# A hybrid decoder block on one core: the order of copies and exponentials in cross attention, xo weights split on Pool, an earlier row load, and down's sums on VectorE

## Chip, core and metric

The kernel runs on one core of a Trainium2 chip. The metric is the device time of one launch in microseconds (us), the median of the runs. TensorE is called PE here, VectorE DVE, ScalarE ACT, GpSimd Pool, and SyncE, which issues nearly all DMAs, SP.

## What is computed

One layer (DEPTH = 1) with sequence 1024 and width 1024, all float32, in three sub-layers, each with an RMSNorm before and after and a residual. Only the second and the third are touched.

```python
def memory_cross_attention(h, mem_n, w_xq, w_xkv, w_xo):   # 4 heads of 256, 256 memory tokens
    q = (h @ w_xq).reshape(bsz, seq, 4, 256)
    k, v = _split(mem_n @ w_xkv, (1024, 1024))
    ...
    s = jnp.einsum('bshd,bmhd->bhsm', q, k) * (256 ** -0.5)
    p = jax.nn.softmax(s, axis=-1)
    o = jnp.einsum('bhsm,bmhd->bshd', p, v).reshape(bsz, seq, 1024)
    return o @ w_xo

def swiglu(h, w_gu, w_down):                               # hidden 2816
    gate, up = _split(h @ w_gu, (2816, 2816))
    return (jax.nn.silu(gate) * up) @ w_down

    ...
    x = x + rms_norm(merged @ w_mix_out[l], g_post_mix[l])
    h = rms_norm(x, g_pre_xa[l])
    mem_n = rms_norm(mem, g_mem[l])
    x = x + rms_norm(memory_cross_attention(h, mem_n, w_xq[l], w_xkv[l], w_xo[l]), g_post_xa[l])
    h = rms_norm(x, g_pre_ffn[l])
    x = x + rms_norm(swiglu(h, w_gu[l], w_down[l]), g_post_ffn[l])
```

## The kernel before

**Arithmetic.** A float32 operand is held as two parts: `hi`, the operand copied into a tile of type float32r, and `lo`, the operand less `hi`. A product is three matmuls: hi by hi, hi by lo, lo by hi (`mm3`, `acc3`). So nearly every operand costs one copy (`hi_sb`: ACT for "a", Pool for "p", DVE for "v") and one subtraction (`lo_of`, L122, on DVE unless another engine is named). Where two operands are split together, one instruction covers both.

The large products (q, gate and up, and down) are taken as 2 x 2 blocks with seven products in place of eight (Strassen's scheme in Winograd's form). Their operands are sums and differences of blocks, formed before the split.

**Cross attention.** A chunk is 128 rows of the sequence; there are eight. `soft(c)` computes a chunk's scores, two heads at a time into one PSUM tile (`sc`, four buffers). DVE takes the maximum (TENSOR_REDUCE) and scales it (TENSOR_SCALAR on two elements), ACT takes two exponentials with their sums. `normed` divides a chunk's probabilities by their sums (a reciprocal and one multiplication of 1024 elements). `turn_(half, h)` transposes the probabilities of a head for four chunks through PSUM (`tr`, two buffers), and ACT and DVE split them. `mix(half, h)` multiplies them with the values into PSUM banks (`mm`, two buffers), and ACT (copy) and DVE (subtraction) split the result `h`. The order is soft 0 to 5, turn (0,0), soft 6, turn (0,1), soft 7, and then mix of one head and turn of the head after the next by turns. In this stretch, and in the lead-ins below, `in_turn(True)` makes DVE, ACT and PE keep the order in which the program lists their work (line 49 is the helper that issues it). Elsewhere a scheduler orders each engine's queue when the kernel is built.

The output projection `out_proj` needs the eight row blocks of `w_xo`, split by `xo_weight(k)` with two buffers for the raw rows (`wraw`). Blocks 0 to 3 are split on Pool ahead of the scores. Blocks 4 to 7 go into the place of the queries (`qP`), and come last in the program, on ACT and DVE.

**Output projection and lead-in.** `out_proj` runs twice, for two halves of four chunks. A chunk loads its row of x, multiplies, takes the mean square (ACT), the reciprocal root (Pool, `rstd`), scales (DVE, L1457), adds the row (L1459), stores, normalises for the next sub-layer, and transposes. The last chunk's generator `run` is left in the list `late`, and the next sub-layer's `lead_in` runs its steps between the first products of that sub-layer. Its first step is the load of its row of x. `behind(marks)` makes an instruction issue after the marked ones. The weights' quarters come by `load` and `more`, one DMA of 512 KB each, on SP.

**Down.** The hidden width is 22 blocks of 128. Blocks 0 and 1, and 20 and 21, are multiplied plainly (`plain`, on operands from `whole_rows`). The other 18 go in three calls of `group`, each with three pairs of blocks. A group runs the products 1, 5, 6, 3, 7, 2, 4 in this order. A product has 36 matmuls on 12 combinations of pair and chunk, after which `add_to` (L2165) adds the PSUM banks to the result `a` on DVE. `operands` forms the sums (`sf`, five buffers) on Pool (L2071 to L2087; in the first group half of those of products 5 and 6 on DVE) and splits them into `op` (six buffers, so two products). The raw blocks lie in `gr` and `dr`, four buffers each. `last_tiles` loads and splits blocks 20 and 21 (`ol`) in the third group, before its product 3. `done` and `finish` are the last normalisation and the store.

Of the kernel before, what the change touches and what calls it, by code (L numbers as in the profile page):

```python
# [54 lines left out]
def hybrid_block(ctx, tc, a, out, dbg=None):  # L55
# [1552 lines left out]
    def lead_in(hb, xf, pa, pb, q, nq, sfp, swp, y, n00, ny, last, nlast, open_ps, open_tx, loaded):  # L1608
# [46 lines left out]
        with behind([loaded]):  # L1655
            next(run)
# [76 lines left out]
    with ExitStack() as q2:  # L1733
# [12 lines left out]
        with ExitStack() as xs:  # L1746
            sfp = pool(xs, "qsf", 4, side="right")
            swp = pool(xs, "qsw", 6, side="right")
            psl = ExitStack()

            def open_tx():
                q1.close()
                return pool(xs, "qtx", 2, side="right")

            def open_ps():
                psx.close()
                return pool(psl, "psl", 1, PSUM)

            def load(q, kh, c0):
                loads.append(quarter_load(q, w_xq, kh, c0 * P))  # L1760
                return quarter(q)

            def more(kh, c0):
                with behind(loads[-1:]):
                    return load(mk(t4, [P, S], F32, "x4"), kh, c0)

            loads = []
            spare = [qP[i].rearrange("p b s -> p (b s)")[:, HALF:HALF + S] for i in (3, 2, 0, 1)]
            n11, n12, q12, q21 = [load(r, kh, c0) for r, (kh, c0) in zip(spare, ((0, 4), (1, 4), (1, 0), (0, 2)))]
            lead_in(hx, xf, xa, xb, (lambda: more(0, 0), q12, q21, lambda: more(1, 2)), (n11, n12, lambda: more(0, 6), lambda: more(1, 6)), sfp, swp,  # L1770
                    rows_of(0), [qT[4 + p][:, 0:HALF] for p in range(2)], lambda: rows_of(4), fourth(2), fourth(6), open_ps, open_tx, loads[-1])
            psl.close()
# [17 lines left out]
        def xo_weight(k, hi_eng, lo_eng):  # L1790
            raw = mk(wbig, [P, D], F32, "wraw", 2)
            nc.sync.dma_start(raw, a["w_xo"][0][k * P:(k + 1) * P, :])
            hi_sb(wxo[k][:, 0], raw, hi_eng)
            lo_of(wxo[k][:, 1], raw, wxo[k][:, 0], lo_eng)

        for k in range(KT // 2):
            xo_weight(k, "p", G)
# [4 lines left out]
        sums, todo = {}, []  # L1802
# [7 lines left out]
        def soft(c):  # L1810
            mx = mk(stats, [P, 4], F32, "mx", bufs=4)
            sums[c] = mk(stats, [P, 4], F32, "sm", bufs=4)
            for h2 in range(2):
                ps = mk(psm, [P, 2, ML], F32, "sc", 4)
                for j in range(2):
                    h = 2 * h2 + j
                    for k in range(2):
                        T.matmul(ps[:, j, :], qT[2 * h + k][:, c * P:(c + 1) * P], kT[:, 2 * h + k, :], start=k == 0, stop=k == 1)
                m = mx[:, 2 * h2:2 * h2 + 2]
                V.tensor_reduce(m, ps, mybir.AxisListType.X, ALU.max)  # L1820
                V.tensor_scalar(m, m, -sc, None, ALU.mult)
                for j in range(2):
                    h = 2 * h2 + j
                    A.activation(prob[c][:, h, :], ps[:, j, :], AF.Exp, scale=sc, bias=mx[:, h:h + 1], accum_out=sums[c][:, h:h + 1])
                if h2 == 0:
                    normed()
            todo.append(c)
# [3 lines left out]
        def turn_(half, h):  # L1831
            for mt in range(2):
                pt = mk(psm, [P, HALF], F32, "tr")
                for ci in range(4):
                    T.transpose(pt[:, ci * P:(ci + 1) * P], prob[half * 4 + ci][:, h, mt * P:(mt + 1) * P], ident)
                t = mk(ptp, [P, 2, HALF], F32R, "pT") if h % 2 else mk(ld, [P, 2, HALF], F32R, "sw")
                A.activation(t[:, 0], pt, AF.Copy)
                V.tensor_tensor(t[:, 1], pt, t[:, 0].bitcast(F32), ALU.subtract)
                pT[half, h, mt] = t[:, 0], t[:, 1]
            normed()  # L1840

        def mix(half, h):
            for d in range(2):
                kk = 2 * h + d
                po = bank()
                for mt in range(2):
                    mm3(po, vh[mt][:, kk * P:(kk + 1) * P], vl[mt][:, kk * P:(kk + 1) * P], *pT[half, h, mt], mt == 0, mt == 1)
                hi, lo = ox[half][kk // 4]
                A.activation(hi[:, kk % 4, :], po, AF.Copy)
                V.tensor_tensor(lo[:, kk % 4, :], po, hi[:, kk % 4, :].bitcast(F32), ALU.subtract)  # L1850
                normed()
# [8 lines left out]
        soft(7)  # L1860
        steps = [(half, h) for half in range(2) for h in range(4)]
# [4 lines left out]
        wxo += [mk(qp, [P, 2, D], F32R, f"bw{k}") for k in range(KT // 2, KT)]  # L1866
        for k in range(KT // 2, KT):
            xo_weight(k, "a", V)
# [29 lines left out]
    with ExitStack() as q4:  # L1898
# [45 lines left out]
        n11 = load(fg[:, 0], 0, 2 * P)  # L1944
        q12 = more(1, 0)
# [7 lines left out]
        def later_results():  # L1953
# [4 lines left out]
                y, n00, later_results, both_gated(y, 0, "xk0"), both_gated(ny, 2, "xk1"), open_ps, open_tx, loads[-1])  # L1958
# [17 lines left out]
    with ExitStack() as q5:  # L1976
# [62 lines left out]
        def group(fs, first, end=None):  # L2039
            raws = []  # L2040
            for f in fs:
                raws.append((mk(rw, [P, 2, S], F32, "gr"), mk(rw, [P, 2, D], F32, "dr")))
                for r, src in zip(raws[-1], (gu_d, w_dn)):
                    if first:
                        nc.sync.dma_start(r[:, 0, 0:HALF], src[f * P:(f + 1) * P, 0:HALF])
                    else:
                        nc.sync.dma_start(r, rows(src, f, 2))
            if first:
                for f, rs in zip(fs, raws):
                    for r, src in zip(rs, (gu_d, w_dn)):  # L2050
                        nc.sync.dma_start(r[:, 0, HALF:], src[f * P:(f + 1) * P, HALF:])
                        nc.sync.dma_start(r[:, 1, :], src[(f + 1) * P:(f + 2) * P, :])
            lo_, hi_ = slice(0, HALF), slice(HALF, S)
            quarter = {}
            for i, (g, d) in enumerate(raws):
                quarter[i] = dict(a11=g[:, 0, lo_], a21=g[:, 0, hi_], a12=g[:, 1, lo_], a22=g[:, 1, hi_],
                                  b11=d[:, 0, lo_], b12=d[:, 0, hi_], b21=d[:, 1, lo_], b22=d[:, 1, hi_])

            E_ = V if first else G
# [4 lines left out]
            def operands(i, nm):  # L2064
                q = quarter[i]
                o = mk(op, [P, 2, 2, HALF], F32R, "op")
                if nm == "1":
                    src = q["a11"], q["b11"]
                elif nm == "5":
                    t = q["5"] = tmp()  # L2070
                    G.tensor_tensor(t[:, 0], q["a21"], q["a22"], ALU.add)  # L2071
                    E_.tensor_tensor(t[:, 1], q["b12"], q["b11"], ALU.subtract)
                    src = t
                elif nm == "6":
                    t = q["6"] = tmp()
                    G.tensor_tensor(t[:, 0], q["5"][:, 0], q["a11"], ALU.subtract)
                    E_.tensor_tensor(t[:, 1], q["b22"], q["5"][:, 1], ALU.subtract)
                    src = t
                elif nm == "3":
                    t = q["3"] = tmp()  # L2080
                    G.tensor_tensor(t[:, 0], q["a12"], q["6"][:, 0], ALU.subtract)
                    G.tensor_tensor(t[:, 1], q["b21"], q["6"][:, 1], ALU.subtract)
                    src = t[:, 0], q["b22"]
                elif nm == "7":
                    t = tmp()
                    G.tensor_tensor(t[:, 0], q["a11"], q["a21"], ALU.subtract)
                    G.tensor_tensor(t[:, 1], q["b22"], q["b12"], ALU.subtract)  # L2087
                    src = t
                elif nm == "2":
                    src = q["a12"], q["b21"]  # L2090
                elif nm == "4":
                    src = q["a22"], q["3"][:, 1]
# [33 lines left out]
            product(pa_, "6", False, False, [(0, 1)])  # L2126
            if end is None:
# [7 lines left out]
            tiles = end()  # L2135
# [41 lines left out]
        def rstd_c(c):  # L2177
            if c % 2 == 0:
                xts3[c // 2] = mk(rw, [P, 2, D], F32, ["gr", "dr"][c // 2 % 2])
# [12 lines left out]

        def last_tiles():
            f = NF - 2
            raws = mk(rw, [P, 2, S], F32, "gr"), mk(rw, [P, 2, D], F32, "dr")
            for r, src in zip(raws, (gu_d, w_dn)):
                nc.sync.dma_start(r, rows(src, f, 2))
            return [whole_rows([r[:, j] for r in raws]) for j in range(2)]

        gpost = load_gain(gpool, "g_post_ffn")  # L2200
        for g0 in range(NFIRST, NF - 2, 6):
            group([g0, g0 + 2, g0 + 4], g0 == NFIRST, last_tiles if g0 + 6 == NF - 2 else None)
# [31 lines left out]
```

## Time and profile before

| | |
|---|---|
| median of 3 runs | 2535.71 us (2533.68 to 2536.29) |
| the profiled execution: time, span | 2529.79 us, 2528.0 us |
| busy: PE, DVE, ACT, Pool | 97%, 72%, 46%, 32% of the span |
| cross attention from the first scores | about 1714 to 1781 us of the span |
| its output projection | about 1781 to 1872 us |
| lead-in of FFN, gate and up | 1872 to 2297 us |
| down | 2297.5 to 2528 us |

A matmul of 512 columns starts 0.227 us after the one before it when PE never waits. Rows of instructions give the start in us from the span's beginning, the duration, the engine, the line, the operation, the tiles as out<-in, shapes, and in square brackets the engine's idle time before the instruction with what ended it. "x2" means that two instructions are merged into one row.

### The profile page before, as it was taken

What the parts mean: (1) busy time and instruction counts of PE and PEld (TensorE: products, weight loads), DVE (VectorE), ACT (ScalarE), POOL (GpSimd) and SP (SyncE); (2) the same over time, 40 slices, a digit from 0 to 9 for tenths busy, and PEclk for the clock granted to TensorE, in tenths of its full rate; (3) what the DMA queues carried; (4) which work ended last, traced back from release to release, by engine and by line L of the source; (5) the groups of instructions that cost most, each with busy time, mean ns of one, the idle gap of its engine ahead of it and who ended that gap; (6) DMA issues with size and microseconds to landing.
All of it is one profiled execution on the core that took longest, in us unless ns stands there. A gap on an engine that the chain in (4) does not pass through costs nothing. (4 is left out here: it accounts for less than half of the span.)

```text
span 2528.0 us, 33414 instructions
## 1 busy us (share of the span) xinstructions
PE 2450.5 (97%) x12306; PEld 2015.0 (80%) x12306; DVE 1809.3 (72%) x2179; ACT 1166.4 (46%) x2076; POOL 821.4 (32%) x639
## 2 busy tenths in 40 slices
PE   7999999999999999989999999999999999999998
PEld 5788888888787878877787788887878888888876
DVE  7665877767587877689888674576468556565997
ACT  5343455555565665566544312344335333334343
POOL 3221545443111211246556141101112322323672
PEclk9999999999999999999999999999999999999999
DMA  7431443333543443265332471321232322224232
GB/s 249 155 117 52 139 146 104 105 100 94 165 104 97 107 110 93 88 204 188 110 97 74 156 265 55 135 99 34 100 134 69 99 76 88 88 92 158 100 133 100
DMA packets 249133, 295.62 MB, mean 117 GB/s; under 512 B 17023, under 2 KB 169096, under 8 KB 248842
## 3 DMA queue, kind: packets, MB, share of 16 engines
q1 hardware_dynamic: 248682, 292.45, 36.9%
q8 instruction: 97, 1.59, 0.3%
q10 hardware_dynamic: 288, 1.05, 0.1%
q14 instruction: 66, 0.54, 0.1%
HBM read 202.20 MB, written 74.45 MB: 109 GB/s over the span
## 5 line engine op out<-in xcount | busy, mean ns | idle before, releaser
L911 DVE TENSOR_TENSOR_SCAN n<-n,mask 128x128 f32<-128x128 f32 (+7 forms) x128 | 189.8, 1508 | 24.1 <-ACT n L910 22.8
L122 DVE TENSOR_TENSOR sw<-sf,sw 128x512 fp32r<-128x512 f32 x142 | 129.9, 918 | 69.7 <-ACT sw L119 67.6
L119 ACT ACTIVATE sw<-sf 128x512 fp32r<-128x512 f32 x142 | 88.9, 628 | 156.1 <-PE mm L230 138.9
L928 ACT ACTIVATE wth<-tr,mone 128x512 fp32r<-128x512 f32 x192 | 110.7, 585 | 83.1 <-PE tr L925 81.2
L929 DVE SCALAR_TENSOR_TENSOR wtl<-tr,wth 128x512 fp32r<-128x512 f32 x192 | 99.6, 543 | 48.0 <-ACT wth L928 48.0
L173 POOL TENSOR_SCALAR rstd<-ms 128x1 f32<-128x1 f32 x74 | 27.0, 365 | 313.6 <-ACT x L180 232.1
L196 POOL TENSOR_TENSOR sf<-wr,wr 128x512 f32<-128x512 f32 x36 | 52.6, 1461 | 231.6 <-DMA wr<-in_w_gu_dram 82.3
L693 DVE SCALAR_TENSOR_TENSOR b<-b,prmT,b 128x1023 f32<-128x1023 f32 (+2 forms) x72 | 109.6, 1522 | 16.9 <-ACT b L687 16.3
L122 DVE TENSOR_TENSOR sw<-wr,sw 128x512 fp32r<-128x512 f32 x107 | 99.2, 929 | 24.3 <-ACT sw L119 24.2
L115 POOL TENSOR_SCALAR v<-va 128x512 fp32r<-128x512 f32 x16 | 20.6, 1291 | 286.1 <-PE av L938 165.7
L229 PE MATMUL mm<-h,sw 128*128 128x512 f32 x288 | 112.0, 389 | 0.0
L230 PE MATMUL mm<-h,sw 128*128 128x512 f32 x288 | 111.7, 389 | 0.0
L910 ACT ACTIVATE n<-sc 128x512 f32<-128x512 f32 (+1 forms) x192 | 88.6, 494 | 46.1 <-PE tr L925 28.8
L228 PE MATMUL mm<-h,sw 128*128 128x512 f32 x288 | 109.9, 389 | 0.0
L125 PE MATMUL mm<-oth,bw 128*128 128x512 f32 x256 | 104.2, 407 | 3.4 <-DVE a L1250 3.4
L125 PE MATMUL p<-bw,h 128*128 128x512 f32 x256 | 100.1, 392 | 1.7 <-DVE x L1457 1.7
L126 PE MATMUL mm<-otl,bw 128*128 128x512 f32 x256 | 101.2, 395 | 0.0
L127 PE MATMUL mm<-oth,bw 128*128 128x512 f32 x256 | 101.1, 395 | 0.0
L127 PE MATMUL p<-bw,h 128*128 128x512 f32 x256 | 100.2, 392 | 0.5 <-DVE h L122 0.5
L126 PE MATMUL p<-bw,h 128*128 128x512 f32 x256 | 100.0, 390 | 0.0
L925 PE MATMUL tr<-ident,n 128*128 128x128 f32 x576 | 95.5, 275 | 3.8 <-DVE wtl L929 3.8
L119 ACT ACTIVATE zh<-zr 128x512 fp32r<-128x512 f32 x72 | 45.0, 630 | 104.8 <-PE ma L492 52.3
(672 smaller groups left out, 7936.1 us busy)
## 6 DMA issues: line engine op xcount, KB each, us to landing
wr<-in_w_in_dram SPq DMA_DIRECT2D x36, 512.0 KB
wr<-in_w_gu_dram SPq DMA_DIRECT2D x72, 256.0 KB
zr<-in_w_in_dram SPq DMA_DIRECT2D x28, 512.0 KB
wraw<-in_w_in_dram SPq DMA_DIRECT2D x20, 512.0 KB
gu_d<-t SPq DMA_DIRECT2D x36, 256.0 KB
zs_d<-zo SPq DMA_DIRECT2D x32, 256.0 KB
xs_d<-b SPq DMA_DIRECT2D x32, 256.0 KB
kl<-gt SPq DMA_DIRECT2D x64, 128.0 KB
```

The costliest lines, as they stand in the source:

```text
L119: A.activation(o, i, AF.Copy)
L122: eng.tensor_tensor(o, i, hi.bitcast(F32), ALU.subtract)
L125: first = T.matmul(ps, sh, mh, start=start, stop=False)
L126: T.matmul(ps, sh, ml, start=False, stop=False)
L127: T.matmul(ps, sl, mh, start=False, stop=stop)
L228: T.matmul(ps, w[0][:, k, :], bh, start=first and k == 0, stop=False, skip_group_check=True)
L229: T.matmul(ps, w[0][:, k, :], bl, start=False, stop=False, skip_group_check=True)
L230: ins = T.matmul(ps, w[1][:, k, :], bh, start=False, stop=last and k == 3, skip_group_check=True)
L693: V.scalar_tensor_tensor(acc[:, sh:], y[:, :S - sh], cw(3 - sh, f), acc[:, sh:], ALU.mult, ALU.add)
L911: V.tensor_tensor_scan(nt[:, 0:L][:, ::-1], nt[:, 0:L][:, ::-1], mask[:, S - L:][:, ::-1], 1.0, ALU.mult, ALU.max)
L928: A.activation(wh[:, t0 * P:], pt[:, t0 * P:], AF.Identity, bias=mone)
L929: V.scalar_tensor_tensor(wl[:, t0 * P:], pt[:, t0 * P:], -1.0, wh[:, t0 * P:].bitcast(F32), ALU.add, ALU.subtract)
```

## The change

It has five parts.
- In `soft`, the exponentials of a chunk's second pair of heads are kept back in a list `exps`. They are issued by the next `soft`, or by the next `turn_` or `mix` behind its ACT copies (in `mix`, behind the first of its two). `normed` is called no longer in `turn_`, and in `mix` once, behind both subtractions. `turn_` makes both transposes and both copies before its two subtractions.
- Blocks 4 to 7 of `w_xo` are split on Pool like the first four, and this comes in the program before the mix loop.
- The load of the last row of x is issued behind the loads listed so far where `lead_in` is called: for xq the four it was behind before, in FFN one instead of five.
- In `group` all sums go to DVE. A pair's raw blocks lie in one tile of eight pieces (`raw_room`, tag `gd`, four buffers), so that products 1 and 2 are split, and the sums of 3 and 7 formed, by one instruction over two pieces in place of two instructions.
- `last_tiles` is called in the first group, behind product 6, and fills the list `last_ops`.

```diff
-    def lead_in(hb, xf, pa, pb, q, nq, sfp, swp, y, n00, ny, last, nlast, open_ps, open_tx, loaded):
+    def lead_in(hb, xf, pa, pb, q, nq, sfp, swp, y, n00, ny, last, nlast, open_ps, open_tx):
...
         late.clear()
-        with behind([loaded]):
-            next(run)
         next(run)
...
             n11, n12, q12, q21 = [load(r, kh, c0) for r, (kh, c0) in zip(spare, ((0, 4), (1, 4), (1, 0), (0, 2)))]
+            with behind(loads):
+                next(late[1])
             lead_in(hx, xf, xa, xb, (lambda: more(0, 0), q12, q21, lambda: more(1, 2)), (n11, n12, lambda: more(0, 6), lambda: more(1, 6)), sfp, swp,
-                    rows_of(0), [qT[4 + p][:, 0:HALF] for p in range(2)], lambda: rows_of(4), fourth(2), fourth(6), open_ps, open_tx, loads[-1])
+                    rows_of(0), [qT[4 + p][:, 0:HALF] for p in range(2)], lambda: rows_of(4), fourth(2), fourth(6), open_ps, open_tx)
             psl.close()
...
-        def xo_weight(k, hi_eng, lo_eng):
+        def xo_weight(k):
             raw = mk(wbig, [P, D], F32, "wraw", 2)
             nc.sync.dma_start(raw, a["w_xo"][0][k * P:(k + 1) * P, :])
-            hi_sb(wxo[k][:, 0], raw, hi_eng)
-            lo_of(wxo[k][:, 1], raw, wxo[k][:, 0], lo_eng)
+            hi_sb(wxo[k][:, 0], raw, "p")
+            lo_of(wxo[k][:, 1], raw, wxo[k][:, 0], G)
...
         for k in range(KT // 2):
-            xo_weight(k, "p", G)
+            xo_weight(k)
...
         prob = [pbt[c // 2][:, c % 2] for c in range(NCH)]
-        sums, todo = {}, []
+        sums, exps, todo = {}, [], []
+        def second_exps():
+            while exps:
+                exps.pop()()
...
         def soft(c):
+            second_exps()
             mx = mk(stats, [P, 4], F32, "mx", bufs=4)
...
+            def exponentials(h2, ps):
+                for j in range(2):
+                    h = 2 * h2 + j
+                    A.activation(prob[c][:, h, :], ps[:, j, :], AF.Exp, scale=sc, bias=mx[:, h:h + 1], accum_out=sums[c][:, h:h + 1])
...
                 V.tensor_scalar(m, m, -sc, None, ALU.mult)
-                for j in range(2):
-                    h = 2 * h2 + j
-                    A.activation(prob[c][:, h, :], ps[:, j, :], AF.Exp, scale=sc, bias=mx[:, h:h + 1], accum_out=sums[c][:, h:h + 1])
                 if h2 == 0:
+                    exponentials(h2, ps)
                     normed()
+            exps.append(lambda ps=ps: exponentials(1, ps))
             todo.append(c)
...
         def turn_(half, h):
-            for mt in range(2):
-                pt = mk(psm, [P, HALF], F32, "tr")
+            pts = [mk(psm, [P, HALF], F32, "tr") for _ in range(2)]
+            ts = [mk(ptp, [P, 2, HALF], F32R, "pT") if h % 2 else mk(ld, [P, 2, HALF], F32R, "sw") for _ in range(2)]
+            for mt, (pt, t) in enumerate(zip(pts, ts)):
                 for ci in range(4):
                     T.transpose(pt[:, ci * P:(ci + 1) * P], prob[half * 4 + ci][:, h, mt * P:(mt + 1) * P], ident)
-                t = mk(ptp, [P, 2, HALF], F32R, "pT") if h % 2 else mk(ld, [P, 2, HALF], F32R, "sw")
                 A.activation(t[:, 0], pt, AF.Copy)
+            second_exps()
+            for mt, (pt, t) in enumerate(zip(pts, ts)):
                 V.tensor_tensor(t[:, 1], pt, t[:, 0].bitcast(F32), ALU.subtract)
                 pT[half, h, mt] = t[:, 0], t[:, 1]
-            normed()
...
                 A.activation(hi[:, kk % 4, :], po, AF.Copy)
+                second_exps()
                 V.tensor_tensor(lo[:, kk % 4, :], po, hi[:, kk % 4, :].bitcast(F32), ALU.subtract)
-                normed()
+            normed()
...
         soft(7)
+        wxo += [mk(qp, [P, 2, D], F32R, f"bw{k}") for k in range(KT // 2, KT)]
+        for k in range(KT // 2, KT):
+            xo_weight(k)
         steps = [(half, h) for half in range(2) for h in range(4)]
...
                 turn_(*steps[i + 2])
-        wxo += [mk(qp, [P, 2, D], F32R, f"bw{k}") for k in range(KT // 2, KT)]
-        for k in range(KT // 2, KT):
-            xo_weight(k, "a", V)
         in_turn(False)
...
         n11 = load(fg[:, 0], 0, 2 * P)
+        with behind(loads):
+            next(late[1])
         q12 = more(1, 0)
...
         lead_in(hw, xf, fa, fb, (lambda: load(fw[:, 0], 0, 0), q12, q21, lambda: q22), (n11, n12, lambda: load(fw[:, 1], 0, FFN + 2 * P), lambda: more(1, FFN + 2 * P)), sfp, swp,
-                y, n00, later_results, both_gated(y, 0, "xk0"), both_gated(ny, 2, "xk1"), open_ps, open_tx, loads[-1])
+                y, n00, later_results, both_gated(y, 0, "xk0"), both_gated(ny, 2, "xk1"), open_ps, open_tx)
         psl.close()
...
-        def group(fs, first, end=None):
+        def raw_room():
+            t = mk(rw, [P, 8, HALF], F32, "gd")
+            return t, [t[:, 4 * i:4 * i + 4].rearrange("p (j h) s -> p j (h s)", j=2) for i in range(2)]
+        def group(fs, first, end=None, early=None):
             raws = []
             for f in fs:
-                raws.append((mk(rw, [P, 2, S], F32, "gr"), mk(rw, [P, 2, D], F32, "dr")))
-                for r, src in zip(raws[-1], (gu_d, w_dn)):
+                raws.append(raw_room())
+                for r, src in zip(raws[-1][1], (gu_d, w_dn)):
                     if first:
...
             if first:
-                for f, rs in zip(fs, raws):
+                for f, (_, rs) in zip(fs, raws):
                     for r, src in zip(rs, (gu_d, w_dn)):
...
                         nc.sync.dma_start(r[:, 1, :], src[(f + 1) * P:(f + 2) * P, :])
-            lo_, hi_ = slice(0, HALF), slice(HALF, S)
             quarter = {}
-            for i, (g, d) in enumerate(raws):
-                quarter[i] = dict(a11=g[:, 0, lo_], a21=g[:, 0, hi_], a12=g[:, 1, lo_], a22=g[:, 1, hi_],
-                                  b11=d[:, 0, lo_], b12=d[:, 0, hi_], b21=d[:, 1, lo_], b22=d[:, 1, hi_])
-            E_ = V if first else G
+            for i, (t, _) in enumerate(raws):
+                quarter[i] = dict(a11=t[:, 0], a21=t[:, 1], a12=t[:, 2], a22=t[:, 3], b11=t[:, 4], b12=t[:, 5], b21=t[:, 6], b22=t[:, 7],
+                                  ab1=t[:, 0:5:4], ab2=t[:, 2:7:4], plus7=t[:, 0:8:7], less7=t[:, 1:6:4])
...
                 if nm == "1":
-                    src = q["a11"], q["b11"]
+                    src = q["ab1"]
                 elif nm == "5":
                     t = q["5"] = tmp()
-                    G.tensor_tensor(t[:, 0], q["a21"], q["a22"], ALU.add)
-                    E_.tensor_tensor(t[:, 1], q["b12"], q["b11"], ALU.subtract)
+                    V.tensor_tensor(t[:, 0], q["a21"], q["a22"], ALU.add)
+                    V.tensor_tensor(t[:, 1], q["b12"], q["b11"], ALU.subtract)
                     src = t
...
                     t = q["6"] = tmp()
-                    G.tensor_tensor(t[:, 0], q["5"][:, 0], q["a11"], ALU.subtract)
-                    E_.tensor_tensor(t[:, 1], q["b22"], q["5"][:, 1], ALU.subtract)
+                    V.tensor_tensor(t[:, 0], q["5"][:, 0], q["a11"], ALU.subtract)
+                    V.tensor_tensor(t[:, 1], q["b22"], q["5"][:, 1], ALU.subtract)
                     src = t
...
                     t = q["3"] = tmp()
-                    G.tensor_tensor(t[:, 0], q["a12"], q["6"][:, 0], ALU.subtract)
-                    G.tensor_tensor(t[:, 1], q["b21"], q["6"][:, 1], ALU.subtract)
+                    V.tensor_tensor(t, q["ab2"], q["6"], ALU.subtract)
                     src = t[:, 0], q["b22"]
...
                     t = tmp()
-                    G.tensor_tensor(t[:, 0], q["a11"], q["a21"], ALU.subtract)
-                    G.tensor_tensor(t[:, 1], q["b22"], q["b12"], ALU.subtract)
+                    V.tensor_tensor(t, q["plus7"], q["less7"], ALU.subtract)
                     src = t
                 elif nm == "2":
-                    src = q["a12"], q["b21"]
+                    src = q["ab2"]
                 elif nm == "4":
...
             product(pa_, "6", False, False, [(0, 1)])
+            if early is not None:
+                early()
             if end is None:
...
-            tiles = end()
+            tiles = end
             product(pc_, "3", False, False, [(0, 1)], lambda ps, c: plain(ps, tiles, c, 1, False), lambda c, _: done(c, 1))
...
             if c % 2 == 0:
-                xts3[c // 2] = mk(rw, [P, 2, D], F32, ["gr", "dr"][c // 2 % 2])
+                if c % 4 == 0:
+                    xts3["room"] = raw_room()[1]
+                xts3[c // 2] = xts3["room"][c // 2 % 2]
                 nc.sync.dma_start(xts3[c // 2], rows(x3_d, c, 2))
...
+        last_ops = []
...
             f = NF - 2
-            raws = mk(rw, [P, 2, S], F32, "gr"), mk(rw, [P, 2, D], F32, "dr")
+            raws = raw_room()[1]
             for r, src in zip(raws, (gu_d, w_dn)):
                 nc.sync.dma_start(r, rows(src, f, 2))
-            return [whole_rows([r[:, j] for r in raws]) for j in range(2)]
+            last_ops.extend(whole_rows([r[:, j] for r in raws]) for j in range(2))
...
         for g0 in range(NFIRST, NF - 2, 6):
-            group([g0, g0 + 2, g0 + 4], g0 == NFIRST, last_tiles if g0 + 6 == NF - 2 else None)
+            group([g0, g0 + 2, g0 + 4], g0 == NFIRST, last_ops if g0 + 6 == NF - 2 else None, last_tiles if g0 == NFIRST else None)
```

## The prediction

> **What bounds the kernel now.** I read the page's busy times first, then the list of what TensorE (PE) waited for, then the stretches of the last stage, and only then single instructions around each wait.
>
> ```profile
> span 2528.0 us, 33414 instructions
> PE 2450.5 (97%) x12306; PEld 2015.0 (80%) x12306; DVE 1809.3 (72%) x2179; ACT 1166.4 (46%) x2076; POOL 821.4 (32%) x639
> ```
>
> PE is busy for all but 77.5 us. The change removes no matmul, so it can only shorten PE's waits, and only those in the stages that it touches. The waits there, from the list for PE (total us, times, longest):
>
> ```profile
> PE mm L49 <- DVE h L49: 3.7, 1, 3.7
> ...
> PE mm L49 <- DVE x L49: 3.3, 1, 3.3
> ...
> PE dna L2112 <- DVE op L122: 3.3, 3, 2.4
> ...
> PE p L125 <- DVE x L1457: 1.7, 1, 1.7
> ...
> PE tr L49 <- DVE sw L49: 1.0, 1, 1.0
> PE dnb L2112 <- DVE op L122: 0.9, 1, 0.9
> PE dnb L2111 <- DVE a L2165: 0.8, 1, 0.8
> ```
>
> Cross attention holds 3.7 + 1.0, its output projection 1.7, FFN's lead-in 3.3, the down product 3.3 + 0.9 + 0.8 = 5.0: in all 14.7 us. That is the most the change can win, 0.6% of the span. About 0.2% (5.1 us) is what a measurement of this kernel can tell from no change.
>
> **Cross attention: copies ahead of the second exponentials.** Timeline of the stage, DVE, ACT and PE:
>
> ```profile
> 1739.09 1.29 DVE L49 TENSOR_TENSOR sw<-tr,sw 128x512 fp32r<-128x512 f32 x2 [1.64 <-ACT sw L49]
> ...
> 1745.09 1.29 DVE L49 TENSOR_TENSOR pT<-tr,pT 128x512 fp32r<-128x512 f32 x2 [1.77 <-ACT pT L49]
> ...
> 1750.45 1.10 ACT L49 ACTIVATE h<-mm 128x512 fp32r<-128x512 f32 x2
> ...
> 1751.09 0.69 DVE L49 TENSOR_TENSOR h<-mm,h 128x512 fp32r<-128x512 f32 x1 [1.77 <-ACT h L49]
> ...
> 1751.84 4.63 PE L49 MATMUL mm<-pT,xk 128*128 128x512 f32 x12 [3.66 <-DVE h L49]
> ```
>
> Three times VectorE (DVE) stands idle for an ACT copy, 1.64 + 1.77 + 1.77 = 5.2 us, because the copy is queued behind the exponentials of the chunk's last two heads. PE then waits for DVE's subtraction, which frees a PSUM bank. The change keeps the DVE work ahead of 1751.09 the same in amount (four maxima, two normalisations, five subtractions) but puts the copy ahead of those exponentials. DVE then loses the 5.2 us of idle time, and PE's 3.7 + 1.0 = 4.7 us can go. The exponentials have cover: their scores have four PSUM buffers, two to a chunk, and nothing needs them before the next chunk's normalisation. Were that cover gone, the price is one DVE wait of about 1.7 us, the size of those above.
>
> **The xo weights k = 4..7 on Pool, before the mix loop.** ACT and DVE lose their part of this splitting; Pool gets four times a copy and a subtraction. The same pair ran on Pool for k = 0..3, and shows what it does to DVE:
>
> ```profile
> 1715.80 2.35 POOL L122 TENSOR_TENSOR bw<-wraw,bw 128x1024 fp32r<-128x1024 f32 x1
> ...
> 1716.31 1.86 DVE L49 TENSOR_SCALAR mx<-mx 128x2 f32<-128x2 f32 x1
> ...
> 1718.25 1.05 POOL L115 TENSOR_SCALAR bw<-wraw 128x1024 fp32r<-128x1024 f32 x1
> ...
> 1723.73 0.17 DVE L49 TENSOR_SCALAR mx<-mx 128x2 f32<-128x2 f32 x1
> ```
>
> A two-element scaling takes 0.17 us alone, and 1.86 us when it ends with Pool's subtraction (1718.17 against 1718.15). The new Pool work, 4 x (1.05 + 2.35) = 13.6 us, starts when the first half of chunk 7's scores is done, which is inside the stretch just repaired. Three DVE instructions ahead of the first freed bank can be blocked: chunk 7's two scalings and chunk 6's normalisation. Each waits from 0 to 2.35 us; I take half, 1.1, for each, so 3.2 lost of 4.7 and 1.5 us kept. The ends are 4.7 (none blocked) and 4.7 - 7.0 = -2.3 (all fully). [...]
>
> Against this stands the output projection:
>
> ```profile
> 1791.12 1.06 ACT L49 ACTIVATE bw<-wraw 128x1024 fp32r<-128x1024 f32 x1 [1.78 <-DMA wraw<-in_w_xo_dram]
> ...
> 1799.44 1.28 DVE L1457 SCALAR_TENSOR_TENSOR x<-p,rstd,g_post_xa 128x1024 f32<-128x1024 f32 x1 [6.00 <-POOL rstd L174]
> ```
>
> The last xo row is split only at 1791. PE fills the time with chunk 1's products, so chunk 0 ends late and chunk 2 waits 1.7 us for its bank. With all eight rows ready some 15 us before the projection, chunk 0 runs in one piece and its rescaling hides under chunk 1: 1.7 us gone. Bounds: 1.7, and 0 if rows 6 and 7 still land late. Pool's next task, the first rstd, comes after the projection's first chunk, so nobody queues behind.
>
> **The last row load.** FFN's lead-in:
>
> ```profile
> 1870.51 0.37 SPq L1578 DMA_DIRECT2D fg<-in_w_gu_dram  x1
> ...
> 1873.55 1.17 SPq L1453 DMA_DIRECT2D x<-x_d  x1
> ...
> 1874.52 1.15 ACT L49 ACTIVATE sw<-fg 128x512 fp32r<-128x512 f32 x2 [6.95 <-DMA fg<-in_w_gu_dram]
> ...
> 1877.66 1.28 DVE L49 SCALAR_TENSOR_TENSOR x<-p,rstd,g_post_xa 128x1024 f32<-128x1024 f32 x1 [1.19 <-POOL rstd L174]
> ...
> 1881.88 1.23 DVE L49 TENSOR_TENSOR x<-x,x 128x1024 f32<-128x1024 f32 x1 [2.94 <-DMA x<-x_d]
> ...
> 1886.88 1.06 PE L49 MATMUL mm<-ident,x 128*128 128x128 f32 x8 [3.27 <-DVE x L49]
> ```
>
> Row 7 of x is issued behind five weight loads and lands 8.3 us later, at 1881.88. The first of the weight loads takes 4.0 us (1870.51 to 1874.52). Issued second, at about 1870.9, the row should land by about 1876 to 1877, before DVE is free for it at 1878.94. The DVE wait of 2.94 us goes, and everything behind it, the transposes included, moves up by that: 2.9 us. What is late next is the chain DVE, ACT, Pool, DVE itself, which leaves PE 0.3 us. The four loads passed on SP's queue come about 1.5 us later; the first of them is split only after that chain. Bounds: 0 (the order does not change) to 3.3. In the xq lead-in the row stays behind all four loads: nothing there.
>
> **Down: sums on DVE.** Stretches of its three groups (the clock stays 1.00), then groups by shape and single instructions:
>
> ```profile
> core 0: us, PE busy (x) PEld busy (x) DVE busy (x) ACT busy (x) POOL busy (x), PEclk, DMA share, GB/s
> ...
> 2319.60:2376.80 57.20, 57.20 (x254) 47.35 (x253) 48.84 (x58) 23.09 (x36) 35.70 (x22) 1.00 0.32 120
> 2376.80:2434.80 58.00, 57.39 (x254) 47.19 (x253) 56.26 (x64) 23.99 (x36) 43.14 (x24) 1.00 0.28 109
> 2434.80:2518.60 83.80, 79.36 (x345) 64.13 (x344) 73.49 (x91) 29.98 (x57) 41.01 (x31) 1.00 0.24 88
> ```
>
> ```profile
> L122 DVE TENSOR_TENSOR op<-sf,op 128x1024 fp32r<-128x1024 f32 x26 | 41.5, 1615 | 5.1 <-ACT op L119 5.1
> ...
> L2082 POOL TENSOR_TENSOR sf<-dr,sf 128x512 f32<-128x512 f32 x9 | 18.5, 2058 | 0.0
> ...
> L122 DVE TENSOR_TENSOR ol<-gr,ol 128x1024 fp32r<-128x1024 f32 x2 | 4.0, 2017 | 0.0
> ```
>
> ```profile
> 2321.40 2.36 DVE L122 TENSOR_TENSOR op<-sf,op 128x1024 fp32r<-128x1024 f32 x2 [1.27 <-ACT op L119]
> ...
> 2324.88 1.29 POOL L2082 TENSOR_TENSOR sf<-dr,sf 128x512 f32<-128x512 f32 x1
> ...
> 2325.95 0.69 DVE L2165 TENSOR_TENSOR a<-a,dnb 128x512 f32<-128x512 f32 x1 [2.18 <-PE dnb L2113]
> ...
> 2331.86 1.21 DVE L122 TENSOR_TENSOR op<-sf,op 128x1024 fp32r<-128x1024 f32 x1
> 2333.00 1.87 DVE L2165 TENSOR_TENSOR a<-a,dna 128x512 f32<-128x512 f32 x3
> ```
>
> Pool's sum of 512 takes 1.29 us alone and 2.06 on average; DVE's subtraction of 1024 takes 1.21 alone and 1.62 on average. So the two block each other, and a group's sums (24 x 1.29 = 31 us) and DVE's subtractions are nearly one queue. In a row, a second 1024 adds 2.36 - 1.21 = 1.15 us, and each further 512 adds (1.87 - 0.69)/2 = 0.59, say 0.6. Before, per block: 3 x 1.15 + 8 x 0.6 = 8.25 of subtractions; a group of three has 24.8, plus Pool's 31: 55.8 us of shared queue, in 57.2 of PE.
>
> After, per block: subtractions 5 x 1.15 + 4 x 0.6 = 8.15 (products 1 and 2 become one strided piece each), sums 4 x 0.6 + 2 x 1.15 = 4.7. A group: 3 x 12.85 + 28 accumulations x 0.6 = 55.4 us on DVE alone. PE gives 57.2/7 = 8.2 us to a product. Products 5, 6, 3 and 7 want about 9.4 each from DVE (3.5 subtractions, 3.5 sums, 2.4 accumulations): 4.8 us too much; 2, 4 and 1 want about 5.9 and give 6.9 back. Operands stand one product ahead, and the first sums can be formed early. So PE nearly keeps running. The last tiles' four subtractions (two of them 4.0 us here) move from group three, where most of PE's waits lie, to group one at 1.15 each, where the sums of the first product are done before PE starts. Their loads join the opening loads. Group two's first block loses its spare buffer and loads only after product 4's operands are formed, about one product (8 us) before it is needed: covered.
>
> I leave 2 of the 5.0 us of waits: 3.0 won. Bounds: 5.0 won, and a loss of 10 (below). [...]
>
> **Sum.** 1.5 + 1.7 + 2.9 + 3.0 = 9.1 us. The profiled execution took 2529.79 us (2528.0 of span and 1.8 around it), so 2520.7 for its like. The median of the runs is 2535.71, 5.9 above it: 2526.6 us.
>
> **Rivals.**
> [...] Chance 0.18.
> (2) Slower: DVE becomes the bound of down. If each instruction costs its single duration (1.21 and 0.69), a group needs 3 x (5 x 1.21 + 4 x 0.69 + 4 x 0.69 + 2 x 1.21) + 28 x 0.69 = 61.3 us against 57.2. Three groups and the last tiles' 4.8 make about 15 us of waits where there were 5: 10 lost, 6.1 won elsewhere, so 3.9 slower, plus 1.5 if attention gives nothing: 2539.6 to 2541.1. It decides from about 0.62 us per 512 on, where 55.4 grows to 57.2. For it: DVE is already at 56.26 of 58 in group two. Against: the row of three. Chance 0.12. [...]
> (3) The scheduler leaves row 7 behind the weights: 6.2 us won, 2529.5. Against: the new code holds it behind one load only. Chance 0.08.
>
> The forecast has the remaining 0.62. Its own range is 5.1 to 14.7 won, 2521.0 to 2530.6. The range 2520.0 to 2537.0 takes in rivals 1 and 3 with a microsecond or two of scatter, and leaves out rival 2 and the odd end. Faster by over 0.2%: 0.62 + 0.08 = 0.70. Same: 0.18. Slower: 0.12.
>
> **What would show it.** Right: PE's wait for h falls from 3.7 towards 1 to 2 us; the waits at 1798 and 1883 are gone, with the x load the second issue after fg; in the down groups Pool is nearly idle, op<-sf has a mean near 1.2 us, and PE waits under 3 us in all. Wrong: DVE scalings of nearly 2 us beside Pool's bw work and mix starting no earlier; or PE waiting for op in each of the three groups while DVE is never idle.

## The result, and the profile after

The changed kernel took 2517.85 us (median of 4 runs, 2516.72 to 2519.81), the kernel before 2534.69 us beside it; ratio 0.9937 (95% interval 0.992 to 0.9954). That is faster, as forecast, but by 16.8 us and not 9.1, and 2517.85 lies below the stated range (2520 to 2537). Another set of runs put it at 2516.01 against 2530.62 (`e9_again`: ratio 0.9945, 0.9933 to 0.9958). The three later sets put the kernel before at 2530.85, 2529.1 and 2530.62, so its first runs were some 4 us on the high side. The profiled executions differ by 13.0 us of span.

The page's head after:

```profile
span 2515.0 us, 33312 instructions
...
PE 2449.4 (97%) x12306; PEld 2016.7 (80%) x12306; DVE 1803.6 (72%) x2205; ACT 1161.5 (46%) x2054; POOL 720.2 (29%) x581
```

What PE waited for in the stages touched (total, times, longest):

```profile
PE mm L49 <- DVE h L49: 4.1, 1, 4.1
...
PE mm L49 <- DVE x L49: 0.4, 1, 0.4
```

The projection's wait and all of down's waits, in the list before under op and a, are gone. The wait of 1.0 for sw is gone too, but the 3.7 us for h has become 4.1.

PE's order of matmuls is the same in nearly all places, so the time between two matmuls of the same number in its sequence (8700, 9090, 9300, 9700, 11350, and the last) gives each stage's time. The stages ahead differ by 1.1 us without any change of order, and what comes after the last matmul by 0.4 us the other way.

| stage (us) | before | after | gained | forecast |
|---|---|---|---|---|
| end of q, attention | 86.59 | 86.34 | 0.25 | 1.5 |
| output projection | 46.98 | 44.84 | 2.14 | 1.7 |
| rest of it, FFN's lead-in | 90.04 | 87.22 | 2.82 | 2.9 |
| gate and up | 375.24 | 375.24 | 0 | 0 |
| down | 223.60 | 216.47 | 7.13 | 3.0 |
| sum | | | 12.34 | 9.1 |

Attention's 0.25 is within the scatter of single profiles: the changed kernel's attention code took 85.56 to 86.93 us in the profiles of `e9_again` and of the experiments that leave it as it is, less when 3.4 us at half clock followed its wait and more when it was 6.8 (see the last section).

Down's three groups after, by stretch:

```profile
core 0: us, PE busy (x) PEld busy (x) DVE busy (x) ACT busy (x) POOL busy (x), PEclk, DMA share, GB/s
2313.40:2370.50 57.10, 57.10 (x253) 47.31 (x252) 56.10 (x73) 26.43 (x33) 0.00 (x0) 1.00 0.38 150
2370.50:2427.70 57.20, 57.20 (x254) 47.35 (x254) 54.53 (x73) 22.03 (x28) 0.00 (x0) 1.00 0.28 110
2427.70:2505.90 78.20, 78.20 (x347) 64.73 (x345) 67.44 (x93) 27.45 (x52) 10.38 (x14) 1.00 0.18 68
```

PE is busy in every microsecond. DVE is busy for 56.1 and 54.5 us of a group, where 55.4 was worked out. Its subtractions lost their blocked time (mean 1615 ns before):

```profile
L122 DVE TENSOR_TENSOR op<-sf,op 128x1024 fp32r<-128x1024 f32 x26 | 31.1, 1233 | 0.2 <-ACT op L119 0.2
```

In FFN's lead-in the row of x is now the second load, and DVE adds it (1.23 us) straight after the scaling:

```profile
1866.97 0.37 SPq L1578 DMA_DIRECT2D fg<-in_w_gu_dram  x1
1867.44 0.45 SPq L1453 DMA_DIRECT2D x<-x_d  x1
...
1874.19 1.28 DVE L49 SCALAR_TENSOR_TENSOR x<-p,rstd,g_post_xa 128x1024 f32<-128x1024 f32 x1 [1.19 <-POOL rstd L174]
1875.51 1.23 DVE L49 TENSOR_TENSOR x<-x,x 128x1024 f32<-128x1024 f32 x1
```

In attention, the new stretch shows why the wait stayed:

```profile
1739.99 2.05 POOL L115 TENSOR_SCALAR bw<-wraw 128x1024 fp32r<-128x1024 f32 x2 [19.42 <-PE sc L49]
1740.28 0.79 DVE L49 TENSOR_SCALAR mx<-mx 128x2 f32<-128x2 f32 x1
...
1742.01 4.71 POOL L122 TENSOR_TENSOR bw<-wraw,bw 128x1024 fp32r<-128x1024 f32 x2
...
1742.87 1.56 DVE L49 TENSOR_SCALAR mx<-mx 128x2 f32<-128x2 f32 x1
...
1744.55 3.26 DVE L49 TENSOR_TENSOR a<-a,sm 128x1024 f32<-128x1024 f32 x1
...
1745.47 0.59 ACT L49 ACTIVATE h<-mm 128x512 fp32r<-128x512 f32 x1
...
1748.13 1.04 POOL L115 TENSOR_SCALAR bw<-wraw 128x1024 fp32r<-128x1024 f32 x1 [1.40 <-DMA wraw<-in_w_xo_dram]
1748.44 0.75 DVE L49 TENSOR_SCALAR mx<-mx 128x2 f32<-128x2 f32 x1
1749.10 0.68 DVE L49 TENSOR_TENSOR h<-mm,h 128x512 fp32r<-128x512 f32 x1
...
1749.83 5.27 PE L49 MATMUL mm<-pT,xk 128*128 128x512 f32 x12 [4.13 <-DVE h L49]
```

The copy of h is done at 1746.06, ahead of the second exponentials, as meant. But chunk 7's first scaling takes 1.56 us in place of 0.17, since it ends only with Pool's first subtraction (1744.43 against 1744.41), and the normalisation behind it 3.26 in place of 1.23, since it stands behind the second one (to 1746.72). Pool's copies hold up two more scalings (chunk 6's second, 0.79, which ends at 1741.07 with a copy at 1741.04, and chunk 7's second, 0.75, at 1749.19 with one at 1749.17). These four lose 0.62 + 1.39 + 2.03 + 0.58 = 4.6 us, and the subtraction that frees the bank waits behind them. Last, the twelve matmuls after the wait take 5.27 us, where 3 are usual (3.13 in e3): the granted clock is about half there (0.53 over the stretch).

```profile
1748.30:1755.10 6.80, 5.27 (x14) 4.11 (x15) 5.24 (x9) 3.08 (x8) 6.63 (x4) 0.53 0.16 63
```

### The profile page after: what moved, and what is told of

Its sections match the earlier page's. It is cut to its first block, busy times and chain, and to the rows that moved or that the text cites. A ratio compares the mean times of both kernels' runs of the same rounds, so it can differ in the third digit from the quotient of the medians.

```text
span 2515.0 us, 33312 instructions
## 1 busy us (share of the span) xinstructions
PE 2449.4 (97%) x12306; PEld 2016.7 (80%) x12306; DVE 1803.6 (72%) x2205; ACT 1161.5 (46%) x2054; POOL 720.2 (29%) x581
## 5 line engine op out<-in xcount | busy, mean ns | idle before, releaser
L122 DVE TENSOR_TENSOR sw<-sf,sw 128x512 fp32r<-128x512 f32 x142 | 129.5, 916 | 69.6 <-ACT sw L119 67.6
```

Of the source, the lines that this page charges most:

```text
L122: eng.tensor_tensor(o, i, hi.bitcast(F32), ALU.subtract)
```

## The experiments

The theory L (the lock): what moved is the blocking between Pool and DVE. Down won 7.1 us because its sums left Pool; attention won nothing because its new order was paid back by Pool's new work beside it. Rivals: chance or shifts from earlier stages (M), DVE's amount of work in attention (W), and the early split and the merged pieces in down (E).

**e1_down: down alone.** Lines of `group` and what it calls from the changed kernel, all else from before.

```diff
-        def group(fs, first, end=None):
+        def raw_room():
+        def group(fs, first, end=None, early=None):
...
-                    G.tensor_tensor(t[:, 0], q["a21"], q["a22"], ALU.add)
-                    E_.tensor_tensor(t[:, 1], q["b12"], q["b11"], ALU.subtract)
+                    V.tensor_tensor(t[:, 0], q["a21"], q["a22"], ALU.add)
+                    V.tensor_tensor(t[:, 1], q["b12"], q["b11"], ALU.subtract)
...
```

> The kernel before with the new down stage alone (sums on VectorE, pieces merged, plain tiles split early). Theory L (the lock: Pool's sums and VectorE's two-input subtractions blocked each other): the three groups run at 57.1 us of TensorE each, the span is 7 us shorter than before's, nothing else moves. Rival M (part of the 7.1 us came from the shift of the stages ahead, or from chance between executions): 3 to 5 us.

2521.66 us, ratio 0.9966 (0.9954 to 0.9978), which is 8.6 us. Down took 216.47 us, as in the changed kernel, with no wait of PE: the 7.1 us belong to this part alone, and M falls. The whole profile was only 3.4 us shorter, where 7 was expected, because its stages ahead ran 1.3 us longer and the lead-in 2.3 us longer, both with unchanged code; the latter is told in the last section.

**e2_xo_late: attention's order without Pool.** Blocks 4 to 7 of w_xo go back to ACT and DVE behind the mix loop.

```diff
-        wxo += [mk(qp, [P, 2, D], F32R, f"bw{k}") for k in range(KT // 2, KT)]
-        for k in range(KT // 2, KT):
-            xo_weight(k)
         steps = [(half, h) for half in range(2) for h in range(4)]
...
                 turn_(*steps[i + 2])
+        wxo += [mk(qp, [P, 2, D], F32R, f"bw{k}") for k in range(KT // 2, KT)]
+        for k in range(KT // 2, KT):
+            xo_weight(k, "a", V)
         in_turn(False)
```

> The changed kernel, but blocks 4 to 7 of w_xo split on ACT and VectorE at the end of the mix loop, as before. Theory L: without Pool's work beside it the new order in attention shows its worth: TensorE's wait for h falls from 4.1 to under 0.7 us, the output projection's wait of 1.7 us (about 2.1 by start times) is back; about 2 us shorter than the changed kernel. Rival W (attention's wait is VectorE's amount of work, which the new order didn't cut): the wait for h stays near 4 us and the kernel is about 2 us longer than the changed one.

2514.27 us, ratio 0.9932 (0.9918 to 0.9946). PE's waits in attention, the projection and FFN's lead-in (the last line, as before the change):

```profile
PE p L125 <- DVE x L1457: 1.7, 1, 1.7
...
PE tr L49 <- DVE sw L49: 0.3, 1, 0.3
PE mm L49 <- DVE sw L49: 0.2, 1, 0.2
```

The wait for h is gone, and W falls. Attention takes 80.67 us, 5.7 less than in the changed kernel; the projection is back at 46.97. The two make 3.5 us, where about 2 were expected: the gain in attention is more than the wait of 4.1, since the half clock behind it is gone too (mean clock 1.00 from 1700 to 1800 us, where the changed kernel has 0.97).

**e3_xo_held: Pool's split, but later.** The four copies on Pool wait for chunk 7's normalisation.

```diff
+        last_norm = [None]
...
+            if mark is not None:
+                tc.add_manual_dep(copied.ins, mark.ins.name,
...
+            if i == 0:
+                wxo += [mk(qp, [P, 2, D], F32R, f"bw{k}") for k in range(KT // 2, KT)]
+                for k in range(KT // 2, KT):
+                    xo_weight(k, last_norm[0])
```

`add_manual_dep` makes Pool's copy wait, by a semaphore, for the marked instruction.

> [...] Theory L: TensorE's wait for h falls from 4.1 to under 0.7 us, the output projection stays without a wait since Pool is done some 15 us before it: 3.6 to 4.1 us shorter than the changed kernel, 2511 us of span. Rival W: no change beyond 0.5 us.

2511.26 us, ratio 0.992 (0.9908 to 0.9932): faster than both kernels. Attention took 80.75, the projection 44.84, the lead-in 86.81, down 216.48 us: 6.0 us less than in the changed kernel, where 3.6 to 4.1 were expected, and 18.3 less than in the kernel before. The stretch:

```profile
1744.29 0.17 DVE L49 TENSOR_SCALAR mx<-mx 128x2 f32<-128x2 f32 x1
...
1744.58 1.23 DVE L49 TENSOR_TENSOR a<-a,sm 128x1024 f32<-128x1024 f32 x1
...
1746.51 0.68 DVE L49 TENSOR_TENSOR h<-mm,h 128x512 fp32r<-128x512 f32 x1
...
1750.37 2.06 POOL L1795 TENSOR_SCALAR bw<-wraw 128x1024 fp32r<-128x1024 f32 x2 [27.77 <-DVE a L49]
...
1752.39 4.78 POOL L122 TENSOR_TENSOR bw<-wraw,bw 128x1024 fp32r<-128x1024 f32 x2
...
1754.41 0.69 DVE L49 TENSOR_TENSOR h<-mm,h 128x512 fp32r<-128x512 f32 x1 [0.60 <-ACT h L49]
```

Scaling and normalisation are back at 0.17 and 1.23 us, and Pool starts at 1750.37, behind the last normalisation (to 1750.22). The splits beside it read one operand from PSUM and keep their 0.68 to 0.69 us, so Pool blocks nothing that PE waits for.

**e8_old_order: Pool's early split with the old order.** `soft`, `turn_` and `mix` as before.

> The changed kernel with the old order of copies, exponentials and normalisations in attention, Pool's split of xo blocks 4 to 7 still ahead of the mix loop. Theory L: the order and the lock are two separate costs: the wait for h grows from 4.1 to 6 us or more and the wait of 1.0 us for sw is back, so the stage is 3 to 4 us longer than in the changed kernel. Rival W (the order is worth nothing): within 1 us of the changed kernel.

2519.26 us, ratio 0.9962 (0.9948 to 0.9976).

```profile
PE mm L49 <- DVE h L49: 6.0, 1, 6.0
PE tr L49 <- DVE sw L49: 0.9, 1, 0.9
```

Attention takes 89.67 us. So the four cases are: old order, no Pool 86.59; new order, no Pool 80.67; old order, Pool early 89.67; new order, Pool early 86.34. The order is worth 5.9 us without Pool's work and 3.3 beside it; that work costs 3.1 and 5.7. These differences hold to about 1 us, since the half clock behind the wait lasted 3.4 us in the first case, 6.8 in the last two, and came in the second not at all.

**e4_sums_pool: down's sums on Pool again,** in the new pieces and with the early split. All of them, while the kernel before had half of those of products 5 and 6 on DVE in the first group.

```diff
-                    V.tensor_tensor(t, q["ab2"], q["6"], ALU.subtract)
+                    G.tensor_tensor(t, q["ab2"], q["6"], ALU.subtract)
```
(and so for the sums of 5, 6 and 7)

> The changed kernel with all of down's sums on Pool (in the new pieces, the plain tiles still split early). Theory L: Pool's sums and VectorE's subtractions block each other again; op<-sf on VectorE goes from 1.23 us back to 1.5 or more, and TensorE waits 4 to 9 us in down. Rival E (the early split of the plain tiles and the merged pieces made the gain): under 2 us of waits.

2525.58 us, ratio 0.9977 (0.9969 to 0.9986), 5.3 us faster than before. Down takes 227.14 us, 10.7 more than with the sums on DVE and 3.5 more than before.

```profile
PE dnb L2126 <- DVE op L122: 5.7, 4, 1.9
PE dna L2126 <- DVE op L122: 1.4, 2, 0.7
```
```profile
L122 DVE TENSOR_TENSOR op<-sf,op 128x1024 fp32r<-128x1024 f32 x26 | 54.3, 2099 | 4.8 <-ACT op L119 4.8
L2097 POOL TENSOR_TENSOR sf<-gd,sf 128x1024 f32<-128x1024 f32 x9 | 27.3, 3049 | 3.0 <-DVE op L122 3.0
```

DVE's subtraction goes from 1.23 to 2.10 us. With the merged pieces and the early split in e4 as in the changed kernel, the engine of the sums alone makes the 10.7 us: E as the cause falls, and what pays is that the sums left Pool. Against the kernel before, e4 differs in more than E: by start times PE lost 4.9, 2.7 and 3.0 us in its three groups, and 0, 0.9 and 5.9 in the kernel before. So group three did gain beside Pool's sums, and group one, where all sums are now Pool's, lost more. No run has the sums on DVE in unmerged pieces; by the spacing of 0.60 and 1.15 us they would add an estimated 0.6 us to a group's 55.4, which still fits.

**e5_tiles_late: the plain tiles split in group three again.**

```diff
-            group(..., last_tiles if g0 == NFIRST else None)
+            group(..., last_tiles if g0 + 6 == NF - 2 else None)
```

> The changed kernel with the plain tiles of down loaded and split in the third group again. Theory L (the lock was down's whole cost): VectorE takes the four subtractions at 1.2 us each beside its sums; TensorE waits at most 1 to 2 us in group three. Rival E (the early split made a good part of the gain): 3 to 5 us of waits in group three.

2514.68 us, ratio 0.9948 (0.9933 to 0.9962). Down takes 216.48 us: no wait at all, where 1 to 2 us were allowed for, so the early split is worth nothing once the sums are on DVE. Group three has the room, since its plain matmuls stretch PE's time to 78.2 us.

**e6_more_sums: is DVE near its bound?** One sum is done twice in each of products 5, 6, 3 and 7.

```diff
+                    V.tensor_tensor(t[:, 0], q["a21"], q["a22"], ALU.add)
                     V.tensor_tensor(t[:, 0], q["a21"], q["a22"], ALU.add)
```

> The changed kernel with one sum of 512 done twice for products 5, 6, 3 and 7 of each pair: 12 more VectorE instructions of 0.6 us in a group, 55.4 + 7.2 = 62.6 us against TensorE's 57.1. If VectorE's queue costs its spacing (0.60 and 1.15 us), TensorE waits about 5 us in each of groups one and two, and 1 to 3 us in group three, 11 to 14 us in all. If each instruction costs its single duration (0.69 and 1.22), the changed kernel would stand at the bound already and the whole 12 x 0.69 = 8.3 us of a group show: 20 us or more.

2527.66 us, ratio 0.9994 (0.9985 to 1.0003). Down takes 227.51 us, 11.0 more.

```profile
2315.00:2375.20 60.20, 57.70 (x253) 47.01 (x252) 59.60 (x80) 23.45 (x31) 0.00 (x0) 1.00 0.31 118
2375.20:2438.20 63.00, 58.38 (x253) 46.91 (x252) 62.39 (x86) 22.50 (x28) 0.00 (x0) 1.00 0.26 100
```

Group two lasts 63.0 us, DVE busy for 62.4 of them, where 62.6 was worked out from the spacing. So DVE's queue costs 0.60 and 1.15 us an instruction, and the changed kernel stands 1.7 us a group under the bound (57.1 less 55.4).

**e7_row_late: the row of x behind five loads again.**

```diff
-        with behind(loads):
-            next(late[1])
         q12 = more(1, 0)
         n12 = load(fg[:, 1], 1, 2 * P)
         q21, q22 = more(0, FFN), more(1, FFN)
+        with behind(loads):
+            next(late[1])
```

> The changed kernel with the last row of x in FFN loaded behind all five weight loads again. Both theories: TensorE's wait for x rises from 0.4 to about 3.3 us, 2.8 us longer; up to 2 us more if a stretch of half clock follows the wait, as it did in e1_down (6.8 us at clock 0.5 behind a wait of 3.2 us).

2519.51 us, ratio 0.9962 (0.9948 to 0.9975). PE's wait for x is 2.4 us and the lead-in 89.22 us, 2.0 longer than in the changed kernel, where 2.8 was expected:

```profile
PE mm L49 <- DVE x L49: 2.4, 1, 2.4
```

The row was issued 2.98 us after the first load (1865.61 to 1868.59), against 3.04 before, and DVE could add it 7.6 us after its issue (1876.15), against 8.3. Why it came sooner stays open. So the position of the load sets the wait, and its size differs between executions by up to 0.9 us.

**e9_again and e10_held_again.**

> The changed kernel once more, beside fresh runs of the kernel before on the same chip. By the stages of the profiles the change is worth 12 to 13 us. If the 16.8 us between the first medians came from a kernel before that ran slow by chance, its median here is 2529 to 2531 and the difference 12 to 14; if the profiles miss something, it stays near 17.

2516.01 us against 2530.62, 14.6 us. That is nearer to the profiles' 12.3 to 13.0 than the first 16.8 was, and its interval (10.6 to 17.0 us) holds all of them.

> The kernel of e3_xo_held once more, beside the changed one on the same chip. By the stages it is 6 us shorter than the changed kernel (5.6 in attention, where the half clock goes with the wait, and 0.4 in the lead-in); without the clock's part it would be 4.1.

2510.49 us, ratio 0.9928 (0.9914 to 0.9941), 5.5 us below the changed kernel on the same chip. Attention took 80.61 against 85.57 us.

## Why the prediction was right, and where it was wrong

The stages won 12.34 us where the sum has 9.1. Down was 4.1 us too small and the projection 0.4, and attention 1.25 too large, which by chance hid a part of it.

*Direction, the row load, the projection.* Right. The row: 2.82 us for 2.9, by the mechanism told. The projection: 2.14 for 1.7; e2 has the wait and 46.97 us back, as told.

*Down* is the term that was mis-sized: 3.0 forecast, 7.13 measured. The demand on DVE was right (55.4 against 54.5 and 56.1), and so was the step that the lead of one product covers products 5, 6, 3 and 7. Two steps failed. First, "I leave 2 of the 5.0 us" was caution with no row behind it; nothing was left. Second, the 5.0 itself: the list counts a wait from the modelled end of a matmul. A matmul is shown with 389 ns but the next starts 227 ns after it, so each wait is listed 0.16 us short, and two waits of 0.2 and 0.3 us are not in the list at all. Behind each wait, too, the second matmul starts some 0.11 us late (0.34 us after the first and not 0.227). By start times down had 7.1 us. The same holds for the cap of 14.7 us: it was not the most that could be won, and e3 won 18.3 in these stages. The two queues that the prediction sets side by side, 55.8 us before and 55.4 after, are not alike either: the first leaves out the 28 accumulations (16.8 us) that the second has.

*Attention* came to 0.25 where 1.5 was forecast, inside the bounds (-2.3 to 4.7). The mechanism was right: Pool blocks DVE (1.56 us in place of 0.17, 3.26 in place of 1.23), and without Pool's work the order is worth 5.9, not 4.7. The step that failed is the 3.2 us for three blocked instructions: four were blocked (chunk 6's second scaling, too), and they lost 4.6. The stretch of half clock after the wait was not in the sum either. So PE's wait for h, which was to fall to 1 to 2 us, rose to 4.1. Of the 7.0 us of full blocking behind the -2.3 end, the four lost 4.6, and the stage came to 0.25. In down PE's waits are gone. Rival 3 did not happen, since the row is the second load.

*Rival 2* (DVE as down's bound) did not happen; e6 shows it, with 7.2 us more of DVE work in a group. Its premise, single durations in a full queue, would make 61.3 + 8.3 = 69.6 us of e6's group and is refuted by the 63.0 us. *The early split* had been counted as a help to group three; e5 shows that it is none once the sums are on DVE.

*The range.* The sum was short by 3.2 us, and it was added to a median of three runs, 2535.71, that was some 5 us above the medians of later runs. The prediction's profile of before had shown 2529.79; its own time was the better base. From 2530.6 the forecast of 9.1 would have been 2521.5, and 12.3 would have been 2518.3, still under the range's lower end of 2520.0. So the base alone doesn't account for the miss: the term for down was needed too.

## What to carry to other kernels

Before work is moved to Pool, list the DVE instructions that run beside it. In these traces those that read two operands from SBUF (a normalisation, 3.26 us in place of 1.23), or scale one (1.56 in place of 0.17), waited for the end of a Pool instruction that had started first; those with an operand in PSUM (0.68) did not. So move the sums to DVE where it has room, and let Pool run where DVE reads PSUM; a wait on a semaphore that starts it some 8 us later (Pool idle for 27.77 us before it, and not 19.42) was worth 5.5 us here. Size PE's waits by the starts of its matmuls, and count the slow clock that followed some waits of 2 us or more here (0.50 for 3.4 or 6.8 us, by estimate 1.2 us lost for each 3.4).

## What the runs showed of the hardware

A wait of PE can be followed by stretches of 3.4 or 6.8 us at half clock. Before, the first mix after the wait of 3.7 us ran so:

```profile
1751.90:1755.30 3.40, 3.40 (x8) 2.72 (x9) 3.02 (x4) 1.13 (x3) 0.00 (x0) 0.50 0.00 0
```

In e1_down it came after the 3.2 us wait in FFN's lead-in (clock 0.50 in the view from 1887.3 to 1894.0), where the kernel before waited 3.3 us without it; the lead-in took 92.38 us in place of 90.04, so by estimate each 3.4 us cost 1.2. In e2 and e3, where attention has no long wait, there is none (mean clock 1.00 from 1700 to 1800 us). In e4 one followed two waits of 0.95 and 2.09 us that lay 2.5 us apart (mean clock 0.97 in its first group).

In each trace the half-clock stretches start whole multiples of 3.413 us apart: in the kernel before at 1082.87, 1164.79, 1250.13 and 1751.89 (24, 25 and 147 times that), in e4 at 1747.37 and 2331.05 (171 times). Lay this grid over the twelve traces from attention on, and count PE's idle time in each of its steps that ran at full clock, from 0.16 us before the shown end of a matmul to the next start. Behind each of the eleven steps with 2.10 us or more the next one ran at half clock (3.37 us in the kernel before, from 1748.47; 2.34 in the changed kernel, from 1744.47); behind none with 1.90 us or less did it. The kernel before's wait in the lead-in lay across two steps, with 1.56 and 1.87 us; of e1_down's, 2.34 us lay in one. So of these two waits, 3.3 and 3.2 us long, one brought the stretch and one did not, by where the grid lay. Ahead of attention, half clock followed steps with 2.06 and 1.96 us in the kernel before (from 1161.38 and 1246.71).

Such stretches in the stages ahead of the change also differ between executions: from two to five times 3.4 us, which is a part of the 5 us by which runs of one kernel differ.
